# Sliding-window attention by whole chunks: both halves' scores together, all transposes together, and PSUM banks shared in turn

## The chip, the cores and the metric

The kernel runs on one core of a Trainium2 chip. Its time is the device time of one launch in microseconds (us). The engines are named as the profile names them: PE (matrix products; PEld is its weight load), DVE (vector), ACT (scalar, activation functions), POOL (a second vector engine) and SP (issues DMAs). Each engine runs its own queue in the order in which the program was laid down; engines meet through semaphores. [...]

## The reference, cut to what matters

One inference step of a one-layer hybrid encoder: retention, sliding-window attention (SWA), cross attention and a gated feed-forward block, on 1024 prompt rows and 64 sample rows, all in float32. The change lies in SWA, whose core is:

```python
SWA_HEADS = 16; SWA_KV_HEADS = 2; SWA_GROUP = 8; SWA_HD = 64; CHUNK = 64; WINDOW = 128

def swa_attend(q, k, v, bias, sinks, valid):
    s = jnp.einsum('bnqhgd,bnkhd->bnhgqk', q, k, preferred_element_type=jnp.float32) * (SWA_HD ** -0.5)
    s = s + bias.astype(jnp.float32)
    if valid is not None:
        s = jnp.where(valid, s, NEG_INF)
    sink = sinks.astype(jnp.float32)[:, :, None, None]
    m = jnp.maximum(jnp.max(s, axis=-1, keepdims=True), sink)
    e = jnp.exp(s - m)
    p = e / (jnp.sum(e, axis=-1, keepdims=True) + jnp.exp(sink - m))
    return jnp.einsum('bnhgqk,bnkhd->bnqhgd', p.astype(v.dtype), v)

a = (rms_norm(ret_o).astype(ret_g.dtype).reshape(B, S, -1) * jax.nn.silu(ret_g)) @ w_ret_out
b = swa_o.reshape(B, S, -1) @ w_swa_out
```

Each chunk of 64 queries sees 192 keys (its own chunk and the two before it; fewer at the start). There are 16 chunks of the prompt and one of the sample: 17.

## The kernel before

The SWA phase (`swa_phase`, `swa`) stands at about 808 to 990 us of the span. A chunk c is worked in two halves (`hf` 0 and 1, eight heads each). In a half, two heads of each of the two key/value groups `v` lie on 128 partitions as rows (head, query), so that a half has four units (v, i), each of 128 rows by up to 192 keys.

- `scores(c, hf)`: PE makes the scores of a half in `pss` (L972; eight rows in the trace, two banks, tag `s`, one buffer). DVE scales them by 0.125 and adds the bias (L982, or L985 for chunks 0 and 1, which have 64 and 128 keys), takes the row maxima (L987), negates and bounds them by the sinks (L988), and forms `es` (L991). ACT takes the exponentials unit by unit with their sums (L993, four times) and that of `es` (L995). DVE makes the reciprocal `den` (L996, L997), POOL multiplies the first 128 keys (L999, `t`) and the last 64 (L1004, `e`).
- `turn(c, hf)`: PE transposes the four units of `t` into `pp` (L1016, one bank, tag `pt0`) and two of `e` into another `pp` (L1027, tag `pt1`); ACT copies the first to SBUF (L1020), DVE the second (L1029). PE also transposes values (L949, copied by ACT at L951).
- `weigh(c)`, after both halves: PE multiplies with the values into `pout` (L1040, sixteen rows in the trace, two banks, tag `out`), and DVE copies the result to `osb` (L1044), which is stored.

Between these blocks PE works on `filler()`, the output projection of the retention branch: `pieces` are groups of three-pass matmuls (L156 to L158, `mm3`, `pd`), each on one of three column ranges (384, 384, 320 columns, `CH`) for one of eight weight units of `w_ret_out`. A unit's float32 weights `raw` are split by ACT (L123) and DVE (L124) into a high and a low part `wq`; the operands `ret` of a column range are split in the same way (`later_operands`, L123 and L124; `first_low`, L1113 to L1125, for the first range). A finished piece is multiplied by its gate on DVE (L1201) and stored.

`fill()` yields how many pieces come at each place: none after the scores of half 0 of chunk 0, six after half 1, then 38 spread over the 34 half steps, then eight. `in_order` ties each block to PE's last matmul, so that the program lays down, for half step i: weigh (if a chunk has ended), scores two halves ahead, turn, filler. Within such constraints a scheduler places every instruction on its engine, also those of the other engines. `step` counts the pieces of the projection; the load of weight unit 2 is issued after `first`, DVE's product of step 2.

Of the kernel before, what the change touches and what calls it, by code (L numbers as in the profile page):

```python
# [19 lines left out]
P = 128  # L20
# [89 lines left out]
class Kernel:  # L110
# [438 lines left out]
    def bias_table(self):  # L549
# [9 lines left out]
        nc.vector.tensor_copy(rb, pb[:16, :256].unsqueeze(1).broadcast_to([16, 2, 256]))  # L559
# [367 lines left out]
    def swa(self, ctx, fill):  # L927
        nc, tc, io = self.nc, self.tc, self.io
        if True:
# [26 lines left out]
            halves = [(c, hf) for c in range(17) for hf in range(2)]  # L956
# [7 lines left out]
            def scores(c, hf):  # L964
                ks, j0, nk = keys(c)
                if hf == 0 and c % 4 == 0 and 0 < c < 13:
                    self.load_queries(qTs, c + 4)
                qT = qTs[c // 4 % 2]
                pss = pw.tile([P, 2, 512], F32, tag="s", name="pss")
# [10 lines left out]
                if nk == NKEY:  # L980
                    fl = lambda x: x.rearrange("p v i n -> p v (i n)")
                    nc.vector.scalar_tensor_tensor(fl(t), pss[:, :, :2 * NKEY], 0.125, fl(bs[:, :, hf]), ALU.mult, ALU.add)  # L982
                else:
                    for v in range(2):
                        nc.vector.scalar_tensor_tensor(t[:, v, :, :nk], ps[:, v, :, :nk], 0.125, bs[:, v, hf, :, j0:],  # L985
                                                       ALU.mult, ALU.add)
                nc.vector.tensor_reduce(nm, t[:, :, :, :nk], AX.X, ALU.max)  # L987
                nc.vector.scalar_tensor_tensor(nm, nm, -1.0, quad(self.minus), ALU.mult, ALU.min)  # L988
# [3 lines left out]
                for v, i in units:  # L992
                    nc.scalar.activation(t[:, v, i, :nk], t[:, v, i, :nk], AF.Exp, bias=nm[:, v, i:i + 1],  # L993
# [14 lines left out]
            def turn(c, hf):  # L1008
                ks, j0, nk = keys(c)
                if hf == 0:  # L1010
                    live[c] = [values(ks + k0) for k0 in ((0, 64, P) if nk == NKEY else (0,))]
                (t, e), vt = live.pop((c, hf)), live[c]
                n = min(P, nk)
                pp = pw.tile([P, 512], F32, tag="pt0", name="pp")
                for j, (v, i) in enumerate(units):
                    self.last_mm = nc.tensor.transpose(pp[:n, j * P:(j + 1) * P], t[:, v, i, :n], self.ident).ins  # L1016
                if hf == 0:
                    live[c, "T"] = [self.pw2.tile([P, 2, 512], F32, tag="pT0", name="pT"), self.pw2.tile([P, 512], F32, tag="pT1", name="pT")]
                pT = live[c, "T"][0][:n]
                nc.scalar.copy(pT[:, :, hf * 256:(hf + 1) * 256], pp[:n, :].rearrange("p (v i) -> p v i", v=2))  # L1020
                cs = [slice(h * 256, (h + 1) * 256) for h in range(2)]
                parts = [[(h, v, vt[0][:n], pT[:, v, cs[h]]) for h in range(2) for v in range(2)]]
                if nk == NKEY:
                    pp = pw.tile([P, 512], F32, tag="pt1", name="pp")
                    for i in range(2):
                        x = e[:, i].rearrange("p r k -> p (r k)")
                        self.last_mm = nc.tensor.transpose(pp[:, i * P:(i + 1) * P], x, self.ident).ins  # L1027
                    pT = live[c, "T"][1]
                    nc.vector.tensor_copy(pT[:, hf * 256:(hf + 1) * 256], pp[:, :256])  # L1029
# [809 lines left out]
```

## Time and profile before

| what | value |
| --- | --- |
| median of three runs | 2186.65 us (2181.92 to 2186.86) |
| the profiled execution | 2187.39 us |
| its span | 2185.2 us, mean granted clock of PE 0.995 |
| PE busy | 2144.0 us, 98% of the span |
| DVE, ACT, POOL busy | 1566.2, 876.4, 651.6 us |
| SWA phase, 806 to 990 us | 184.00 us, PE busy in 176.75 of them |

A row of the timeline reads: start in us, duration, engine, line and operation, output and inputs with their shape, how many instructions, and in brackets the idle time before it with what ended it. A row of the groups reads: line, engine, operation, shapes and count, then busy time in us and the mean ns of one, then idle time before them with its releasers. The table of stretches has, for each stretch, its length and the busy time of each engine, then the granted clock of PE (PEclk, 1.00 is full), the share of the DMA engines and GB/s.

### The profile page before, as it was taken

How to read it: one execution, taken by the hardware profiler on the slowest of the kernel's cores; microseconds unless marked ns; L12 is line 12 of the kernel's file. 1: busy time of each engine (PE TensorE's matmuls, PEld its weight loads, DVE VectorE, ACT ScalarE, POOL GpSimd, SP SyncE). 2: the span in 40 equal slices, each digit the busy share in tenths (PEclk: the TensorE clock that was granted, in tenths of full speed). 3: DMA queues.
4: the chain of work that ended last, by engine and by line, in shares of the span. 5: the costliest groups of instructions: out<-in, count | busy, mean ns of one | idle time of the engine just before them, and what ended most of it. 6: DMA issues, size and time to landing. Idle time of an engine off the chain costs nothing.

```text
span 2185.2 us, 41707 instructions
## 1 busy us (share of the span) xinstructions
PE 2144.0 (98%) x16389; PEld 2088.9 (96%) x16389; DVE 1566.2 (72%) x2658; ACT 876.4 (40%) x1898; POOL 651.6 (30%) x498
## 2 busy tenths in 40 slices
PE   8999999999999998999999999999999999999997
PEld 8999999999999997889999999999999999999997
DVE  8996968776677658775455555768777776787588
ACT  7343424344344455653233333333322322344243
POOL 1222333332344213340000000014565555514531
PEclk9999999999999999999999999999999999999998
DMA  6434354445244567326443111422333323294333
GB/s 207 157 128 122 109 148 128 133 121 153 103 160 159 171 206 233 124 80 219 121 154 119 43 49 59 146 87 91 122 126 113 104 99 117 93 331 135 127 110 116
DMA packets 181444, 290.83 MB, mean 133 GB/s; under 512 B 40290, under 2 KB 109314, under 8 KB 181250
## 3 DMA queue, kind: packets, MB, share of 16 engines
q1 hardware_dynamic: 176130, 278.18, 39.7%
q10 hardware_dynamic: 4608, 8.36, 1.0%
q8 instruction: 129, 2.11, 0.4%
q0 software_dynamic: 512, 1.64, 0.2%
q14 instruction: 65, 0.53, 0.1%
HBM read 196.95 MB, written 91.16 MB: 132 GB/s over the span
## 4 chain that ended last, share of the span: by engine, by line
PE 78%; DVE 11%; DMA 5%; issue 2%; ACT 2%; POOL 1%; SPq 0%; POOLq 0%; DVEq 0%; ACTq 0%
PE pq L215 16%; PE pq L212 15%; PE pq L213 15%; PE pd L156 7%; PE pd L158 7%; PE pd L157 7%; DVE wq L124 2%; PE pout L1040 1%; PE pss L972 1%; DMA hl<-d_op 1%; DVE u L259 1%; PE pp L1016 1%; DVE T L124 1%; DVE B L124 1%; DMA raw<-w_k 1%
## 5 line engine op out<-in xcount | busy, mean ns | idle before, releaser
L124 DVE TENSOR_TENSOR wq<-raw,wq 128x512 fp32r<-128x512 f32 (+1 forms) x499 | 443.2, 891 | 145.0 <-ACT wq L123 142.9
L123 ACT CAST wq<-raw 128x512 fp32r<-128x512 f32 (+1 forms) x499 | 302.9, 614 | 588.2 <-PE pq L215 210.4
L212 PE MATMUL pq<-T,wq 128*128 128x272 f32 x1832 | 492.1, 288 | 4.9 <-ACT wq L123 3.2
L213 PE MATMUL pq<-T,wq 128*128 128x272 f32 x1832 | 492.9, 289 | 0.0
L213 PE MATMUL pq<-B,wq 128*128 128x272 f32 x1592 | 427.3, 288 | 3.1 <-DVE B L124 2.9
L212 PE MATMUL pq<-B,wq 128*128 128x272 f32 x1592 | 425.9, 288 | 0.7 <-DVE tok L725 0.4
L190 POOL TENSOR_TENSOR raw<-raw 128x512 f32<-128x512 f32 (+1 forms) x59 | 86.5, 1467 | 1030.5 <-DVE rs_r L301 481.0
L215 PE MATMUL pq<-T,wq 128*128 128x272 f32 x1832 | 382.7, 289 | 1.5 <-DVE wq L124 1.5
L212 PEld LDWEIGHTS pq<-T,wq 128*128 128x128 f32 x1832 | 345.0, 188 | 6.8 <-ACT wq L123 3.3
L213 PEld LDWEIGHTS pq<-T,wq 128*128 128x128 f32 x1832 | 344.6, 188 | 1.2 <-issue 1.1
L215 PE MATMUL pq<-B,wq 128*128 128x272 f32 x1592 | 331.5, 289 | 0.0
L213 PEld LDWEIGHTS pq<-B,wq 128*128 128x128 f32 x1592 | 298.8, 188 | 4.5 <-DVE B L124 4.4
L212 PEld LDWEIGHTS pq<-B,wq 128*128 128x128 f32 x1592 | 298.8, 188 | 1.7 <-issue 0.9
L215 PEld LDWEIGHTS pq<-T,wq 128*128 128x128 f32 x1832 | 290.0, 190 | 2.7 <-DVE wq L124 1.8
L215 PEld LDWEIGHTS pq<-B,wq 128*128 128x128 f32 x1592 | 251.5, 189 | 0.5 <-issue 0.4
L259 DVE TENSOR_TENSOR u<-pq,u 128x544 f32<-128x544 f32 x177 | 127.2, 719 | 92.6 <-PE pq L215 92.5
L193 POOL TENSOR_TENSOR raw<-raw 128x512 f32<-128x512 f32 (+1 forms) x59 | 80.8, 1370 | 93.4 <-DVE wq L124 83.5
L598 DVE TENSOR_TENSOR stage<-pq,u 128x544 f32<-128x544 f32 x112 | 80.3, 717 | 36.7 <-PE pq L215 33.9
L191 POOL TENSOR_TENSOR raw<-raw 128x512 f32<-128x512 f32 (+1 forms) x59 | 89.1, 1510 | 3.6
L196 POOL TENSOR_TENSOR raw<-raw 128x512 f32<-128x512 f32 (+1 forms) x59 | 86.0, 1457 | 4.4
L1488 POOL TENSOR_TENSOR stage<-stage,rstd_f 128x544 f32<-128x544 f32 x40 | 63.9, 1608 | 39.1 <-ACT stage L1487 39.1
L156 PE MATMUL pd<-xc,wq 128*128 128x256 f32 (+1 forms) x256 | 74.5, 291 | 0.0
(385 smaller groups left out, 4555.5 us busy)
## 6 DMA issues: line engine op xcount, KB each, us to landing
hl<-d_op SPq DMA_DIRECT2D x85, 272.0 KB, 5.0
d_qkv<-stage SPq DMA_DIRECT2D x44, 272.0 KB, 2.4
d_op<-stage SPq DMA_DIRECT2D x44, 272.0 KB, 2.1
d_op<-ht SPq DMA_DIRECT2D x44, 272.0 KB, 3.1
raw<-w_gate SPq DMA_DIRECT2D x22, 512.0 KB, 3.5
raw<-w_up SPq DMA_DIRECT2D x22, 512.0 KB, 3.5
raw<-w_down SPq DMA_DIRECT2D x16, 512.0 KB, 5.3
d_gate<-stage ACTq DMA_DIRECT2D x28, 272.0 KB, 3.2
```

The costliest lines, as they stand in the source:

```text
L123: self.last_cast = self.nc.scalar.copy(hi, src).ins
L124: return self.nc.vector.tensor_tensor(out=lo, in0=src, in1=hi.bitcast(F32), op=ALU.subtract).ins
L156: mm(ps, wh, xh, start=start, stop=False)
L157: mm(ps, wh, xl, start=False, stop=False)
L158: self.last_mm = mm(ps, wl, xh, start=False, stop=stop).ins
L190: tt(out=a11, in0=a11, in1=a21, op=sub)
L191: tt(out=a21, in0=a21, in1=a22, op=add)
L196: tt(out=a12, in0=a12, in1=a11, op=sub)
L212: mm(ps[:, c, :HC], w[:, 0, ks], x[:, 0, cs], start=start, stop=False)
L213: mm(ps[:, c, :HC], w[:, 0, ks], x[:, 1, cs], start=False, stop=False)
L215: self.last_mm = mm(ps[:, c, :HC], w[:, 1, ks], x[:, 0, c * HC:(c + 1) * HC], start=False, stop=stop).ins
L259: add = lambda out, a, b: nc.vector.tensor_tensor(out=out, in0=a, in1=b, op=ALU.add)
```

## The change

- The scores of both halves of a chunk are issued together, the chunk's transposes together, and the weighing stands ahead of the next scores. For chunk c the program lays down: weigh(c-1), scores(c+1), filler, turn(c), filler.
- Tag `s` has two buffers of two banks each. Scores of a half take one; all eight transposes of `t` of a chunk take the next, as one tile `pp` of two banks. The four transposes of `e` go into the upper half of the `out` tile, whose lower half later takes the weighing; one DVE copy per chunk (`rest`, L1024) takes them out in place of two. Tags `pt0` and `pt1` are gone; the phase uses as many banks as before.
- The first softmax step is one DVE operation per unit, `tensor_tensor_reduce` (L984): sum of scores and bias, times -0.125, with the running minimum kept; it is followed by a readout of one element per partition. It takes the place of L982/L985, L987 and L988. The bias table is stored times 8, and the exponential takes scale -1.
- The load of weight unit 2 is issued after the marks (`ready` and the exponential of `es`) that are the latest at step 6, in place of DVE's product of step 2.

Lines move: L972 becomes L974, L993 L990, L1016 stays, L1020 becomes L1017, L1027 L1020, L1029 L1024, L1040 L1032, L1044 L1036, L1201 L1195.

```diff
-        nc.vector.tensor_copy(rb, pb[:16, :256].unsqueeze(1).broadcast_to([16, 2, 256]))
+        nc.vector.tensor_scalar(rb, pb[:16, :256].unsqueeze(1).broadcast_to([16, 2, 256]), 8.0, None, ALU.mult)
...
-                yield []
                 yield [pieces] * 6
...
-            def scores(c, hf):
+            def scores(c):
+                if c % 4 == 0 and 0 < c < 13:
+                    self.load_queries(qTs, c + 4)
+                for hf in range(2):
+                    half_scores(c, hf)
...
-                pss = pw.tile([P, 2, 512], F32, tag="s", name="pss")
+                pss = pw.tile([P, 2, 512], F32, tag="s", bufs=2, name="pss")
...
-                if nk == NKEY:
-                    fl = lambda x: x.rearrange("p v i n -> p v (i n)")
-                    nc.vector.scalar_tensor_tensor(fl(t), pss[:, :, :2 * NKEY], 0.125, fl(bs[:, :, hf]), ALU.mult, ALU.add)
-                else:
-                    for v in range(2):
-                        nc.vector.scalar_tensor_tensor(t[:, v, :, :nk], ps[:, v, :, :nk], 0.125, bs[:, v, hf, :, j0:],
-                                                       ALU.mult, ALU.add)
-                nc.vector.tensor_reduce(nm, t[:, :, :, :nk], AX.X, ALU.max)
-                nc.vector.scalar_tensor_tensor(nm, nm, -1.0, quad(self.minus), ALU.mult, ALU.min)
+                for v, i in units:
+                    u = quad(self.minus)[:, v, i:i + 1]
+                    nc.vector.tensor_tensor_reduce(t[:, v, i, :nk], ps[:, v, i, :nk], bs[:, v, hf, i, j0:], -0.125, u,
+                                                   ALU.add, ALU.min, nm[:, v, i:i + 1])
...
-                    nc.scalar.activation(t[:, v, i, :nk], t[:, v, i, :nk], AF.Exp, bias=nm[:, v, i:i + 1],
+                    nc.scalar.activation(t[:, v, i, :nk], t[:, v, i, :nk], AF.Exp, bias=nm[:, v, i:i + 1], scale=-1.0,
...
-            def turn(c, hf):
+            def turn(c):
...
-                pp = pw.tile([P, 512], F32, tag="pt0", name="pp")
-                for j, (v, i) in enumerate(units):
-                    self.last_mm = nc.tensor.transpose(pp[:n, j * P:(j + 1) * P], t[:, v, i, :n], self.ident).ins
...
+                pp = pw.tile([P, 2, 512], F32, tag="s", bufs=2, name="pp")
+                po = pw.tile([P, 2, 512], F32, tag="out", name="pout")
+                first = self.pw2.tile([P, 2, 512], F32, tag="pT0", name="pT")[:n]
...
+                for hf in range(2):
+                    t, e = live.pop((c, hf))
+                    for j, (v, i) in enumerate(units):
+                        self.last_mm = nc.tensor.transpose(pp[:n, hf, j * P:(j + 1) * P], t[:, v, i, :n], self.ident).ins
+                    nc.scalar.copy(first[:, :, cs[hf]], pp[:n, hf, :].rearrange("p (v i) -> p v i", v=2))
+                    for i in range(2 if nk == NKEY else 0):
+                        x = e[:, i].rearrange("p r k -> p (r k)")
+                        self.last_mm = nc.tensor.transpose(po[:, hf, (2 + i) * P:(3 + i) * P], x, self.ident).ins
...
+                    nc.vector.tensor_copy(rest.rearrange("p (h i) -> p h i", h=2), po[:, :, 256:])
...
-            for i in range(-2, n):
-                if i > 0:
-                    self.in_order(lambda: weigh(*halves[i - 1]))
-                if i + 2 < n:
-                    self.in_order(lambda: scores(*halves[i + 2]))
-                if i >= 0:
-                    self.in_order(lambda: turn(*halves[i]))
...
+            self.in_order(lambda: scores(0))
...
+            filled()
+            for c in range(17):
+                if c:
+                    self.in_order(lambda: weigh(c - 1))
+                if c < 16:
+                    self.in_order(lambda: scores(c + 1))
+                filled()
+                self.in_order(lambda: turn(c))
+                filled()
...
-                        with tc.issue_after(first):
+                        with tc.issue_after(first[0]), tc.issue_after(first[1]):
...
-                if step == 2:
-                    first = ins
+                if step == 6:
+                    first = self.marks[-1]
```

PE, chunk 0's second half of transposes (`t_9799` before, `t_9796` now), in the kernel before; a row is line, operation, output and inputs with the numbers of their buffers, shape, and in brackets the engines or DMA queues whose semaphores it waits for:

```order
L156 MATMUL pd_9956<-ret3_9728,wq_9888 128x384
L157 MATMUL pd_9956<-ret3_9728,wq_9888 128x384
L158 MATMUL pd_9956<-ret3_9728,wq_9888 128x384
L972 MATMUL pss_9981<-swin0_9711,swin1_9712 128x128 [waits DVE_49,PE_49]
L972 MATMUL pss_9981<-swin0_9711,swin1_9712 128x128 x3
L1016 MATMUL pp_10003<-ident_63,t_9799 64x128 [waits Activation_49,Pool_49]
L1016 MATMUL pp_10003<-ident_63,t_9799 64x128 x3
```

and in the kernel as changed:

```order
L158 MATMUL pd_9967<-ret3_9728,wq_9888 128x384
L948 MATMUL pd_9992<-ident_63,swin5_9716 128x128 [waits DMAHW2_49,DVE_49]
L1016 MATMUL pp_9995<-ident_63,t_9774 64x128 [waits DVE_49,Pool_49]
L1016 MATMUL pp_9995<-ident_63,t_9774 64x128 x3
L1016 MATMUL pp_9995<-ident_63,t_9796 64x128 [waits Activation_49,Pool_49]
L1016 MATMUL pp_9995<-ident_63,t_9796 64x128 x3
L156 MATMUL pd_9967<-ret4_9729,wq_9891 128x384
```

Both groups of transposes now write one tile `pp_9995`, and the second, which waits for ACT's copy of the first, stands directly behind it.

ACT, around the copy of chunk 0's first transposes (`pT_9952` before, `pT_9997` now), in the kernel before:

```order
L123 COPY wq_9888<-raw_9886 128x512 [waits Activation_49]
L123 COPY wq_9891<-raw_9886 128x512 [waits Activation_49]
L123 COPY wq_10499<-raw_10497 128x512 [waits DMAHW1_49,Activation_49]
L123 COPY wq_10502<-raw_10497 128x512 [waits Activation_49]
L951 COPY swin4_9715<-pd_9944 128x128 [waits PE_49]
L1020 COPY pT_9952<-pp_9947 64x2x256 [waits PE_49]
L993 ACTIVATE t_9927,den_9933<-t_9927,nm_9928 128x128 [waits DVE_49]
L993 ACTIVATE t_9927,den_9933<-t_9927,nm_9928 128x128 x3
```

and in the kernel as changed, where row one and two are chunk 1's exponentials:

```order
L990 ACTIVATE t_9927,den_9933<-t_9927,nm_9928 128x128 [waits DVE_49] x4
L990 ACTIVATE t_9949,den_9955<-t_9949,nm_9950 128x128 [waits DVE_49] x4
L992 ACTIVATE es_9934<-es_9934 128x4 [waits DVE_49]
L992 ACTIVATE es_9956<-es_9956 128x4 [waits DVE_49]
L123 COPY ret0_9725<-swin3_9714 128x384 [waits DMAHW7_49]
L123 COPY ret1_9726<-swin3_9714 128x384 [waits DMAHW0_49]
L123 COPY ret2_9727<-swin3_9714 128x384 [waits DMAHW2_49]
L123 COPY ret3_9728<-swin6_9717 128x384 [waits DMAHW3_49]
L123 COPY ret4_9729<-swin6_9717 128x384 [waits DMAHW4_49]
L123 COPY ret5_9730<-swin6_9717 128x384 [waits DMAHW5_49]
L123 COPY ret6_9731<-swin6_9717 128x384 [waits DMAHW7_49,Activation_49]
L950 COPY swin4_9715<-pd_9992 128x128 [waits PE_49]
```

The next row is L1017's copy of the first group. The conversions of unit 2 (`wq_10499`, `wq_10502`) have left this place; they stand behind chunk 2's exponentials and four conversions of `ret`. The copy, which had stood ahead of chunk 1's exponentials, stands behind all eight of them and seven conversions.

PE, a later chunk, where the weighing begins, in the kernel before:

```order
L156 MATMUL pd_10320<-ret7_9732,wq_9752 128x320
L157 MATMUL pd_10320<-ret7_9732,wq_9752 128x320
L158 MATMUL pd_10320<-ret7_9732,wq_9752 128x320
L1040 MATMUL pout_10381<-pT_10312,swin4_9715 64x256 x2
L1040 MATMUL pout_10381<-pT_10312,swin4_9715 64x256 [waits Activation_49]
L1040 MATMUL pout_10381<-pT_10312,swin4_9715 64x256
```

and in the kernel as changed:

```order
L157 MATMUL pd_10327<-ret7_9732,wq_9752 128x320
L158 MATMUL pd_10327<-ret7_9732,wq_9752 128x320
L1016 MATMUL pp_10343<-ident_63,t_10180 128x128 [waits Activation_49]
L1016 MATMUL pp_10343<-ident_63,t_10180 128x128 x3
L1032 MATMUL pout_10344<-pT_10345,swin4_9715 64x256 [waits DVE_49]
L1032 MATMUL pout_10344<-pT_10345,swin4_9715 64x256
L1032 MATMUL pout_10344<-pT_10345,swin4_9715 64x256 [waits Activation_49]
L1032 MATMUL pout_10344<-pT_10345,swin4_9715 64x256
```

Before, filler stood between the last transposes and the weighing; now the second group of transposes stands directly ahead of it, and the weighing's third row waits for ACT's copy of that group.

More of the change, by code (lines that the diff above doesn't have):

```diff
@@ L955, in swa @@
             units = [(v, i) for v in range(2) for i in range(2)]
-            halves = [(c, hf) for c in range(17) for hf in range(2)]
             live, outs = {}, {}
@@ L1006, in scores @@
                 live[c, hf] = t, e
-            def turn(c, hf):
+            def turn(c):
                 ks, j0, nk = keys(c)
-                if hf == 0:
-                    live[c] = [values(ks + k0) for k0 in ((0, 64, P) if nk == NKEY else (0,))]
-                (t, e), vt = live.pop((c, hf)), live[c]
+                vt = [values(ks + k0) for k0 in ((0, 64, P) if nk == NKEY else (0,))]
                 n = min(P, nk)
-                pp = pw.tile([P, 512], F32, tag="pt0", name="pp")
-                for j, (v, i) in enumerate(units):
[L1016 to L1020, printed above, removed]
-                cs = [slice(h * 256, (h + 1) * 256) for h in range(2)]
-                parts = [[(h, v, vt[0][:n], pT[:, v, cs[h]]) for h in range(2) for v in range(2)]]
-                if nk == NKEY:
[L1024 to L1029, printed above, removed]
-                    parts.append([(h, r ^ h, vt[2 - r][rows[r]], pT[rows[r], cs[h]]) for h in range(2) for r in (h, 1 - h)])
-                live[c, "parts"] = parts
@@ new lines, in turn, with weigh @@
+                parts = [[(h, v, vt[0][:n], first[:, v, cs[h]]) for h in range(2) for v in range(2)]]
+                if nk == NKEY:
+                    rest = self.pw2.tile([P, 512], F32, tag="pT1", name="pT")
+                    nc.vector.tensor_copy(rest.rearrange("p (h i) -> p h i", h=2), po[:, :, 256:])
+                    parts.append([(h, r ^ h, vt[2 - r][rows[r]], rest[rows[r], cs[h]]) for h in range(2) for r in (h, 1 - h)])
+                live[c] = parts, po
+            def weigh(c):
+                parts, po = live.pop(c)
```

24 lines of the change are left out of this document (8 added, 16 removed).

## The prediction, made before the changed kernel was run

> **What bounds the kernel now.** I read the busy time of each engine over the whole span first, then the same in stretches of the one phase that the change touches, then PE's list of instructions there, and last ACT's and DVE's where PE stood still.
>
> ```profile
> PE 2144.0 (98%) x16389; PEld 2088.9 (96%) x16389; DVE 1566.2 (72%) x2658; ACT 876.4 (40%) x1898; POOL 651.6 (30%) x498
> core 0: us, PE busy (x) PEld busy (x) DVE busy (x) ACT busy (x) POOL busy (x), PEclk, DMA share, GB/s
> 806.00:820.00 14.00, 12.47 (x90) 11.84 (x88) 7.83 (x22) 12.59 (x36) 4.11 (x8) 0.88 0.56 189
> 820.00:840.00 20.00, 16.10 (x102) 13.61 (x100) 15.06 (x37) 9.42 (x32) 3.73 (x4) 0.91 0.86 281
> 880.00:900.00 20.00, 20.00 (x155) 16.37 (x154) 16.72 (x37) 13.16 (x52) 7.58 (x12) 1.00 0.44 136
> 806.00:990.00 184.00, 176.75 (x1298) 144.64 (x1297) 134.20 (x320) 111.00 (x408) 64.33 (x101) 0.98 0.46 145
> ```
>
> PE bounds it: 98% of the span, and 176.75 of the 184 us of this phase. So the change can win at most 184 - 176.75 = 7.25 us of idle time, the clock lost around it, and the small gaps between blocks. DVE leaves 184 - 134.2 = 49.8 us free, ACT 73. In the later stretch PE never stops. The idle time sits at the start:
>
> ```profile
> 809.67 0.66 PE L972 MATMUL pss<-swin,swin 64*128 64x64 f32 x8 [0.68 <-DVE t L985]
> 822.42 0.71 PE L972 MATMUL pss<-swin,swin 64*128 64x128 f32 x8
> 823.24 0.60 PE L1016 MATMUL pp<-ident,t 128*64 128x128 f32 x4
> 823.59 0.42 PE L156 MATMUL pd<-ret,wq 128*128 128x384 f32 x1
> 825.62 0.34 PE L158 MATMUL pd<-ret,wq 128*128 128x384 f32 x1
> 829.85 0.72 PE L972 MATMUL pss<-swin,swin 64*128 64x128 f32 x8 [3.90 <-DVE t L985]
> 831.46 0.52 PE L157 MATMUL pd<-ret,wq 128*128 128x384 f32 x1
> 834.02 0.41 PE L156 MATMUL pd<-ret,wq 128*128 128x384 f32 x1
> 827.10 1.14 ACT L123 CAST wq<-raw 128x512 fp32r<-128x512 f32 x2 [7.82 <-DMA raw<-w_ret_out]
> 828.96 0.75 DVE L985 SCALAR_TENSOR_TENSOR t<-pss,swin 128x256 f32<-128x256 f32 x2
> ```
>
> The 3.90 us wait is a chain: weight unit 2 came late from memory (ACT waited 7.82 us), DVE's half of that conversion stands in its queue ahead of chunk 1's first softmax step (828.96), and PE needs that step to free its only scores bank. After it eight matmuls took 834.02 - 831.46 = 2.56 us, 0.32 each; the twelve from 823.59 to 825.62 took 2.03/11 = 0.185 each. So about 1.4 us more went to a lower clock (0.91 granted in that stretch).
>
> **What the change removes.** Unit 2's conversions now stand behind chunk 2 in both queues, so 3.90 goes. The second scores bank removes 0.68. The 0.61 below (PE waiting for an ACT copy behind four exponentials) and the POOL waits of 0.84 and 0.31 go too, since chunk c is turned 1.5 chunks after its scores instead of one. Together 3.90 + 1.40 + 0.68 + 0.61 + 1.15 = 7.7 us.
>
> ```profile
> 845.93 0.66 PE L1016 MATMUL pp<-ident,t 128*128 128x128 f32 x4 [0.84 <-POOL t L999]
> 846.89 0.44 PE L1027 MATMUL pp<-ident,e 128*128 128x128 f32 x2 [0.31 <-POOL e L1004]
> 861.84 0.65 PE L1040 MATMUL pout<-pT,swin 128*64 128x256 f32 x4
> 863.11 1.25 PE L1040 MATMUL pout<-pT,swin 128*64 128x256 f32 x12 [0.61 <-ACT pT L1020]
> 862.49 0.56 ACT L1020 COPY pT<-pp 128x512 f32<-128x512 f32 x1
> ```
>
> **What it adds on DVE.** Per half chunk, three operations become four units of a new 192-element operation, each with a one-element readout.
>
> ```profile
> L993 ACT ACTIVATE t<-t,nm 128x192 f32<-128x192 f32 x120 | 53.1, 443 | 25.6 <-DVE nm L988 23.9 <-DVE es L991 1.0 <-DVE den L997 0.7
> L982 DVE SCALAR_TENSOR_TENSOR t<-pss,swin 128x768 f32<-128x768 f32 x30 | 28.6, 952 | 5.1 <-PE pss L972 4.9
> L987 DVE TENSOR_REDUCE nm<-t 128x4 f32<-128x768 f32 x30 | 28.3, 943 | 0.0
> L988 DVE SCALAR_TENSOR_TENSOR nm<-nm,minus 128x4 f32<-128x4 f32 x34 | 5.7, 168 | 0.6
> L985 DVE SCALAR_TENSOR_TENSOR t<-pss,swin 128x256 f32<-128x256 f32 x4 | 1.5, 416 | 0.0
> L985 DVE SCALAR_TENSOR_TENSOR t<-pss,swin 128x128 f32<-128x128 f32 x4 | 1.0, 286 | 0.0
> L987 DVE TENSOR_REDUCE nm<-t 128x4 f32<-128x512 f32 x2 | 1.4, 685 | 0.1
> L987 DVE TENSOR_REDUCE nm<-t 128x4 f32<-128x256 f32 x2 | 0.8, 420 | 0.1
> ```
>
> No row shows the operation. From L985, 128 more elements cost 416 - 286 = 130 ns, so 156 ns are fixed and 192 elements are 351 ns; the readout is at most like L988's 168. At 519 ns a unit, 136 units are 70.6 us, against 28.6 + 28.3 + 5.7 + 1.5 + 1.0 + 1.4 + 0.8 = 67.3 now. Bounds: at 952/4 + 0 a unit it saves 35 us of DVE, and up to 49.8 us more is covered by DVE's free time. I take nothing on PE's path. Merging the `rest` copies saves DVE a little, likewise covered.
>
> [...]
>
> **What it adds on PE, chunk 0.** Both halves' transposes now write one tile, back to back, and the second four wait until ACT has copied the first four. In between nothing hides that copy, and in ACT's queue it stands behind all eight exponentials of chunk 1 and seven conversions of `ret`.
>
> ```profile
> 822.90 0.54 DVE L1201 TENSOR_TENSOR swin<-pd,swin 128x384 f32<-128x384 f32 x1
> 830.66 0.40 ACT L993 ACTIVATE t<-t,nm 128x128 f32<-128x128 f32 x1 [1.78 <-DVE nm L988]
> 832.21 0.19 ACT L995 ACTIVATE es<-es 128x4 f32<-128x4 f32 x1
> 832.31 1.74 ACT L123 CAST ret<-swin 128x384 fp32r<-128x384 f32 x4
> L951 ACT COPY swin<-pd 128x128 f32<-128x128 f32 x18 | 4.7, 264 | 10.8 <-PE pd L949 10.8
> ```
>
> PE: chunk 1's scores begin at 822.42 - 0.68 = 821.7, take 2 x 0.65, twelve matmuls 2.2, transposes 0.5; the second four are due near 825.7. DVE is busy until 822.90 + 0.54 = 823.4, so the first unit is done near 823.8. DVE makes units at most every 0.45 us and ACT takes them every (832.21 - 830.66)/4 = 0.39, so the eighth exponential ends near 827.3. Then es twice 0.2, seven conversions at 1.74/4 = 0.43, 3.0, a values copy of 0.2 (at most 0.26) and the copy of 0.56 (row 862.49): 831.2. PE waits about 5.5 us (5.0 where DVE's units come quicker than ACT takes them). The lower clock after it, 1.4, I keep as in the kernel before.
>
> **Chunk 1.** The same order returns. From 831.2: transposes 0.45, twelve slower matmuls 3.4, the weighing and both scores halves 1.0 + 1.7, twelve matmuls 2.1, transposes 0.45, so the second four are due at 840.3. The first half's scores are done at 836.8; eight exponentials at 0.443 make 3.5, then the queue holds 0.2, four conversions of 320 columns and unit 2's pair, then the copy:
>
> ```profile
> 845.48 1.52 ACT L123 CAST ret<-swin 128x320 fp32r<-128x320 f32 x4
> 891.80 1.68 PE L1040 MATMUL pout<-pT,swin 128*64 128x256 f32 x16
> 893.40 0.92 PE L972 MATMUL pss<-swin,swin 64*128 64x192 f32 x8
> 894.42 0.60 PE L1016 MATMUL pp<-ident,t 128*128 128x128 f32 x4
> 894.86 0.38 PE L1027 MATMUL pp<-ident,e 128*128 128x128 f32 x2
> 895.11 0.59 ACT L1020 COPY pT<-pp 128x512 f32<-128x512 f32 x1 [0.23 <-PE pp L1016]
> ```
>
> 836.8 + 0.5 + 3.5 + 0.2 + 1.52 + 1.14 + 0.6 = 844.3, a wait of 4.0 us; 2 if the conversions can run early, 5 if their loads land late. The clock after it: 0 to 1.4, I take 1.2.
>
> [...]
>
> **Chunks 2 to 16.** The wait is hidden by matmuls that now stand between the two groups of transposes; but the second group stands straight ahead of the weighing, whose third row reads its copy. From the first of four transposes (894.42) the copy starts after 0.69 (895.11) and takes 0.59, and PE goes on 0.06 after a copy's end (862.49 + 0.56, 863.11): 1.34. PE's next block starts after 0.44 (894.86), and four passes lie before the waiting row at 1.60/16 = 0.10 each (891.80 to 893.40): 0.84. I take the difference, 0.5 us a chunk; bounds 0 (the scheduler's matmuls reach PE earlier) and 0.9 (a conversion of 0.43 queued ahead of the copy). Fifteen chunks: 7.5 us. Against it, one scores block and one transposes block per chunk instead of two each saves a few gaps, 0.1 to 0.2: 17 x 0.13 = 2.2 us.
>
> **The sum.** -7.7 + 5.5 + 1.4 (chunk 0) + 4.0 + 1.2 (chunk 1) + 7.5 - 2.2 = +9.7 us. The profiled execution took 2187.39 us (span 2185.2), 0.74 above the median of the runs, 2186.65. 2187.4 + 9.7 = 2197.1; on the median's footing 2196.4, which I forecast.
>
> **Rivals.**
> 1. Only the early waits come; the copies of later chunks are hidden. Then 9.7 - 7.5 = +2.2: 2188.9. For it: ACT has 73 us free and the copy itself is short. Against: 0.61 us was lost at 863.11 in that place when the copy was late.
> 2. Faster: the two early waits are together under 2.5 us, because ACT starts its conversions before the exponentials are ready or DVE's units are short, and the clock holds; with no waits in later chunks, -7.7 + 2.5 - 2.2 = -7.4: 2179.3. It decides from early waits below 2.5 us. Against it: an engine's queue runs in order, and twelve or more operations stand ahead.
> 3. DVE becomes the bound: a unit with readout at 1.1 us makes 136 x 1.1 = 150 us, 82 more than now against 49.8 free: +32 and some 5 us of the early waits, near 2224. It decides from (67.3 + 49.8)/136 = 0.86 us. Against it: every DVE row here fits 156 ns and 1 ns an element.
> 4. The waits are longer: each ACT copy stands behind one more conversion (0.43 to 0.57) in most of the later chunks, 15 x 0.5 = 7.5: 2204. For it: two conversions of weights come in many chunks, and ACT runs in order. Against: those copies have matmuls of about 4 us ahead of them.
>
> **How the numbers follow.** The likeliest course 0.55 (its own range 2190 to 2203); rival 1 0.14, rival 2 0.13, rival 3 0.06, rival 4 0.12. About 0.3%, 6.6 us, is what a measurement of this kernel tells from no change: faster is below 2180.1, slower above 2193.2. Faster: rival 2, 0.13. Same: rival 1 and a fifth of the likeliest, 0.25. Slower: the rest, 0.62. The range 2181 to 2207 leaves out rival 3, most of rival 2 and a little of rival 4.
>
> **What would show it.** Right: in the changed kernel's PE list a wait of 4 us or more ahead of the second group of L1016 in chunks 0 and 1, released by ACT's L1017, and about 0.5 us ahead of L1032 in most later chunks, with no wait on DVE's scores step near 826. The DVE units at L984 should read about 350 ns. Wrong: units over 0.8 us with PE waiting on DVE at L974; PE's busy time unbroken from 840 on; or the first waits under 2 us, which would make the forecast's sign wrong.

## The result, and the profile after

The changed kernel took 2194.26 us, the median of six runs (2189.27 to 2195.73), against 2185.47 us (2181.92 to 2186.86) for the kernel before in six runs beside them: a ratio of 1.0037, 95% interval 1.0025 to 1.0049. It is slower by 8.8 us, of which the interval allows 5.5 to 10.7. The forecast was 2196.4.

The stretches of the phase after (columns as in the prediction):

```profile
820.00:840.00 20.00, 15.73 (x98) 13.39 (x96) 13.29 (x51) 10.84 (x42) 3.31 (x4) 0.83 0.45 146
840.00:860.00 20.00, 15.77 (x104) 12.46 (x106) 15.40 (x41) 11.06 (x40) 8.95 (x12) 0.91 0.84 267
880.00:900.00 20.00, 19.73 (x152) 16.02 (x149) 12.78 (x60) 11.77 (x48) 7.38 (x12) 1.00 0.38 118
```

In the stretch of 840 to 860 us PE had been busy for 18.85 of the 20 us; now it is for 15.77, and its clock is 0.91. PE's timeline names the waits:

```profile
816.98 0.45 PE L156 MATMUL pd<-ret,wq 128*128 128x384 f32 x1 [1.47 <-ACT swin L1166]
824.74 0.60 PE L1016 MATMUL pp<-ident,t 128*64 128x128 f32 x4
829.54 1.03 PE L1016 MATMUL pp<-ident,t 128*64 128x128 f32 x4 [4.21 <-ACT pT L1017]
843.94 0.63 PE L1016 MATMUL pp<-ident,t 128*128 128x128 f32 x4 [4.00 <-ACT pT L1017]
```

The 3.90 us wait on DVE is gone; in its place PE waits 4.21 and 4.00 us for ACT's copy between the two groups of transposes of chunks 0 and 1. The wait of 1.47 us ahead of them is for L1166, where ACT scales a result of the values projection (816.47, `swin<-pd,mtok`) and so frees its bank of PSUM, which PE writes and ACT reads (the same line is L1172 in the order before). ACT's timeline around chunk 0's copy shows what it stood behind: the last of chunk 1's exponentials, the two of `es`, seven conversions, then the copy.

```profile
825.22 0.39 ACT L990 ACTIVATE t<-t,nm 128x128 f32<-128x128 f32 x1
825.60 0.28 ACT L992 ACTIVATE es<-es 128x4 f32<-128x4 f32 x2
825.79 2.97 ACT L123 CAST ret<-swin 128x384 fp32r<-128x384 f32 x7
828.67 0.25 ACT L950 COPY swin<-pd 128x128 f32<-128x128 f32 x1
828.83 0.58 ACT L1017 COPY pT<-pp 64x512 f32<-64x512 f32 x1
```

PE had reached the second group at about 825.3; without the seven conversions, by an estimate from these rows (825.79 + 829.41 - 828.67), the copy would have been done near 826.5.

In a later chunk (PE's timeline, and ACT's row between):

```profile
876.39 0.60 PE L1016 MATMUL pp<-ident,t 128*128 128x128 f32 x4
876.92 1.99 PE L1032 MATMUL pout<-pT,swin 128*64 128x256 f32 x16
878.84 1.41 PE L974 MATMUL pss<-swin,swin 64*128 64x192 f32 x14
877.03 0.58 ACT L1017 COPY pT<-pp 128x512 f32<-128x512 f32 x1 [1.82 <-PE pp L1016]
```

The weighing takes 878.84 - 876.92 = 1.92 us to the next block, where it took 1.60 before: 0.32 us of waiting. The idle column shows none of it here and at most 0.17 in other chunks; the rest lies within the merged row, which is 1.99 us long where the row of before (891.80) is 1.68. The copy runs from 877.03 to 877.61, within the weighing.

DVE's new operation and its readout, as groups:

```profile
L984 DVE CUSTOM_DVE_ANT_0 t<-pss,swin,minus 128x192 f32<-128x192 f32 x120 | 42.9, 414 | 3.7 <-PE pss L974 3.7
L984 DVE DVE_READ_ACCUMULATOR2_ANT nm<- 128x1 f32 x136 | 11.3, 83 | 0.0
```

Busy time of a row overlaps that of its neighbours: in the timeline the units start 0.34 us apart, readout included (898.34, 898.68, 899.02 in one half).

Below, the phase is measured from the start of the first scores to the start of the last weighing, and cut where the weighing of chunk 2 starts. All numbers are differences of start times in the profiled executions.

| kernel | first scores to chunk 2 | chunk 2 to chunk 16 | sum | median of all runs | ratio to before, 95% |
| --- | --- | --- | --- | --- | --- |
| before | 44.94 | 133.05 | 177.99 | 2185.47 | |
| before, second profile | 43.36 | 133.10 | 176.46 | | |
| changed | 48.69 | 135.05 | 183.74 | 2194.26 | 1.0037 (1.0025 to 1.0049) |
| changed, second profile | 52.24 | 135.14 | 187.38 | | |
| two tiles | 41.69 | 130.97 | 172.66 | 2181.75 | 0.9983 (0.9974 to 0.9992) |
| unit 2 alone | 45.03 | 133.83 | 178.86 | 2184.51 | 1.0004 (0.9993 to 1.0016) |
| old softmax in the new order | 50.40 | 156.69 | 207.09 | 2212.51 | 1.0125 (1.0111 to 1.0138) |
| copies first | 42.40 | 136.71 | 179.11 | 2189.14 | 1.0020 (1.0009 to 1.0032) |
| two tiles and copies first | 38.33 | 133.65 | 171.98 | 2180.57 | 0.9986 (0.9975 to 0.9996) |
| new softmax in the old order | 42.77 | 132.02 | 174.79 | 2183.60 | 0.9997 (0.9988 to 1.0006) |
| old place of unit 2 | 49.38 | 135.00 | 184.38 | 2190.95 | 1.0031 (1.0019 to 1.0042) |
| two tiles, old softmax | 45.90 | 148.40 | 194.30 | 2204.37 | 1.0098 (1.0083 to 1.0114) |
| values' scaling first | 37.13 | 133.76 | 170.89 | 2182.15 | 0.9991 (0.9982 to 0.9999) |

The ratios go by the kernel before, run beside each kernel on the same chip, whose median was 2184.56 beside the first four experiments, 2183.67 beside the next four and 2183.80 beside the last.

### The profile page after: what moved, and what is told of

Same layout as the page of the kernel before. It is cut to its first block, busy times and chain, and to the rows that moved or that the text cites. A ratio compares the mean times of both kernels' runs of the same rounds, so it can differ in the third digit from the quotient of the medians.

```text
span 2193.5 us, 41793 instructions
## 1 busy us (share of the span) xinstructions
PE 2145.9 (98%) x16389; PEld 2092.0 (95%) x16389; DVE 1553.9 (71%) x2809; ACT 873.4 (40%) x1898; POOL 649.8 (30%) x498
## 5 line engine op out<-in xcount | busy, mean ns | idle before, releaser
L124 DVE TENSOR_TENSOR wq<-raw,wq 128x512 fp32r<-128x512 f32 (+1 forms) x499 | 448.7, 903 | 158.2 <-ACT wq L123 156.6
L190 POOL TENSOR_TENSOR raw<-raw 128x512 f32<-128x512 f32 (+1 forms) x59 | 85.2, 1445 | 1040.8 <-DVE rs_r L301 485.1
L193 POOL TENSOR_TENSOR raw<-raw 128x512 f32<-128x512 f32 (+1 forms) x59 | 80.7, 1368 | 93.3 <-DVE wq L124 83.4
L191 POOL TENSOR_TENSOR raw<-raw 128x512 f32<-128x512 f32 (+1 forms) x59 | 87.5, 1484 | 3.6
L196 POOL TENSOR_TENSOR raw<-raw 128x512 f32<-128x512 f32 (+1 forms) x59 | 83.9, 1423 | 4.4
L990 ACT ACTIVATE t<-t,nm 128x192 f32<-128x192 f32 (+2 forms) x136 | 58.8, 434 | 51.6 <-DVE nm L984 51.6
```

Of the source, the lines that this page charges most:

```text
L124: return self.nc.vector.tensor_tensor(out=lo, in0=src, in1=hi.bitcast(F32), op=ALU.subtract).ins
L190: tt(out=a11, in0=a11, in1=a21, op=sub)
L191: tt(out=a21, in0=a21, in1=a22, op=add)
L193: tt(out=a11, in0=a22, in1=a11, op=sub)
L196: tt(out=a12, in0=a12, in1=a11, op=sub)
```

## The experiments

### Two tiles in place of one

```diff
-                pss = pw.tile([P, 2, 512], F32, tag="s", bufs=2, name="pss")
+                pss = [pw.tile([P, 512], F32, tag="s%d" % v, bufs=2, name="pss") for v in range(2)]
...
-                pp = pw.tile([P, 2, 512], F32, tag="s", bufs=2, name="pp")
+                pps = [pw.tile([P, 512], F32, tag="s%d" % hf, bufs=2, name="pp") for hf in range(2)]
```

The same four banks, but each is a tile of its own, so that the second transposes no longer wait for the copy of the first. The scores of a half now lie in two tiles as well.

> The changed kernel with each pair of banks of tag s held as two tiles of one bank, so that the two halves' transposes go to two tiles; all else as changed. Theory (the second transposes wait for ACT's copy of the first because they write one tile): the waits of 4.21 and 4.00 us ahead of L1016 are gone; what remains of them moves to the weighing of chunks 0 and 1 (about 2.9 and 1.8 us, since ACT's copies still stand behind eight exponentials and the conversions); the weighing of later chunks takes 1.60 again in place of 1.92. About 2182 us, 12 less than the changed kernel, some 3 less than the kernel before. Rival (the wait belongs to ACT's queue, not to the shared tile): the same 4 us appear ahead of the weighing and the time stays within 3 us of 2194. Rival (DVE's new operation sets the time): no change.

Measured: 2181.75 us, faster than both kernels, as the theory said. PE's timeline at the weighing of chunk 0, and one later chunk:

```profile
830.04 0.65 PE L1032 MATMUL pout<-pT,swin 64*64 64x256 f32 x4 [1.52 <-ACT pT L1017]
830.93 1.12 PE L1032 MATMUL pout<-pT,swin 64*64 64x256 f32 x4 [0.24 <-ACT pT L1017]
888.05 1.68 PE L1032 MATMUL pout<-pT,swin 128*64 128x256 f32 x16
889.66 1.57 PE L974 MATMUL pss<-swin,swin 64*128 64x192 f32 x16
```

Both 4 us waits are gone, 1.76 us of the first shows up at the weighing (2.9 was expected), none of the second (1.8 was expected), and a later weighing takes 889.66 - 888.05 = 1.61 again. The scheduler also moved the second transposes back ahead of the filler, which now hides the copy. So both the early and the later loss come from the second group's dependence on the first group's copy. Splitting the tile of the scores is not what helped: from chunk 4 to 15 they take 1.50 us a chunk with either.

### Copies ahead of the conversions

```diff
-        with self.tc.issue_after(a), self.tc.issue_after(b):
+        with self.tc.issue_after(a), self.tc.issue_after(b), self.tc.issue_after(self.copied):
...
-            extra = {2: (1, 0), 3: (1, 1), 5: (2, 0), 7: (2, 1)}
+            extra = {3: [(1, 0), (1, 1)], 5: [(2, 0)], 7: [(2, 1)]}
```

`copied` is the last L1017 of a chunk, and the first four conversions are asked for one step later; the shared tile stays.

> The changed kernel with ACT's conversions of ret issued behind the chunk's copies (L1017) in place of ahead of them, the one shared tile kept. Theory (the early waits are the copy's place in ACT's queue): the 4.21 us falls to about 1.1 and the 4.00 to about 1.2, and the lower clock behind each goes, 2184 to 2188 us; the weighing of later chunks still takes 1.92. Rival (the conversions are needed at once by PE, so the wait moves to L156): waits of 2 to 4 us ahead of L156 at chunks 1 and 2 and 2191 us or more.

Measured: 2189.14 us, a little more than expected. Of the changed kernel's loss 3.7 us are back by the ratios (1.0020 beside 1.0037), 5.1 by the medians. The profiled run, 2194.52 us, was the slowest of its twelve. PE's timeline:

```profile
829.85 0.60 PE L1016 MATMUL pp<-ident,t 128*64 128x128 f32 x4 [1.28 <-ACT pT L1017]
839.69 0.63 PE L1016 MATMUL pp<-ident,t 128*128 128x128 f32 x4 [1.16 <-ACT pT L1017]
862.85 0.66 PE L1016 MATMUL pp<-ident,t 128*128 128x128 f32 x4 [1.88 <-ACT pT L1017]
```

The two waits fell to 1.28 and 1.16 as forecast. A new one of 1.88 at chunk 3 and two of 0.78 near 851 us give part of it back. The one long wait ahead of L156, 2.81 us at 820.17, is for L1166 and lies ahead of the conversions that were moved, so that rival falls. The weighing of later chunks still takes 1.93 us. The place in ACT's queue sets how long the early waits are; the shared tile makes them waits at all.

### Both together

> Both experiments before together: two tiles of one bank for the transposes, and ACT's conversions of ret behind the chunk's copies. Theory (the two causes add up to all of the early waits): the waits of 1.52 and 0.24 us at the weighing of chunk 0 that two tiles left go too, later chunks as with two tiles: 2179 us, 2 to 3 less than two tiles alone. Rival (with two tiles the copies are no longer late, and the conversions behind them only make PE's L156 wait): 2182 us or more.

Measured: 2180.57 us, the lowest median of the study, but not to be told from two tiles alone by these intervals. ACT's timeline at chunk 0, then PE's largest wait:

```profile
823.76 1.06 ACT L1017 COPY pT<-pp 64x512 f32<-64x512 f32 x2
824.71 3.41 ACT L123 CAST ret<-swin 128x384 fp32r<-128x384 f32 x8
856.18 1.68 PE L1032 MATMUL pout<-pT,swin 128*64 128x256 f32 x16 [1.67 <-DVE pT L1024]
```

The waits of 1.52 and 0.24 us at chunk 0's weighing are gone, as the theory said. Up to chunk 2 the profile is 3.4 us shorter than that of two tiles, but not by these waits alone: the wait for L1166 is 0.9 us shorter, a stretch of lower clock in the other profile (matmuls 0.32 us apart from 835.33 to 837.57, and 0.175 from 837.78 on) is missing here, and three new waits of 0.78, 0.52 and 0.67 us for DVE's softmax stand ahead of L1016. Up to chunk 16 2.7 us come back, 1.67 of them on DVE's copy of the `e` transposes. The time shows no gain, so the theory's 2 to 3 us did not come.

### Unit 2's load moved, in the order before

```diff
-                        with tc.issue_after(first):
+                        with tc.issue_after(first[0]), tc.issue_after(first[1]):
...
-                if step == 2:
-                    first = ins
+                if step == 6:
+                    first = self.marks[-1]
```

> The kernel before with one part of the change alone: the load of weight unit 2 is issued after the marks of step 6. Theory: the wait of 3.90 us on DVE at chunk 1 and about 1.4 us of lower clock after it go, nothing else moves: 2180 us, 5 less than before. Rival (the wait only moves to the next place that needs DVE or ACT, or to unit 2's first use): within 2 us of 2185.5.

Measured: 2184.51 us against 2184.56: no gain clear of noise (the interval goes from 1.5 us less to 3.5 more). PE's timeline holds what came in place of the 3.90, and ACT's what the longest of the later ones stood behind:

```profile
821.03 0.69 PE L156 MATMUL pd<-ret,wq 128*128 128x384 f32 x1 [2.79 <-ACT swin L1172]
841.62 0.66 PE L1016 MATMUL pp<-ident,t 128*128 128x128 f32 x4 [1.20 <-POOL t L999]
849.38 0.44 PE L156 MATMUL pd<-ret,wq 128*128 128x384 f32 x1 [2.13 <-ACT swin L951]
861.28 0.92 PE L972 MATMUL pss<-swin,swin 64*128 64x192 f32 x8 [0.67 <-DVE t L982]
848.03 1.13 ACT L123 CAST wq<-raw 128x512 fp32r<-128x512 f32 x2
```

The rival holds by the time: the wait goes, and others come. The 2.13 us one ends with L951, which stands right behind unit 2's two conversions in their new place. The 2.79 us one lies ahead of everything that the edit moves; it differs from run to run (nothing and 0.75 us in the two profiles of the kernel before). With it came 2.6 us of lower clock (matmuls 0.32 us apart from 821.52 to 826.96, and 0.175 behind them), and the profiled run, 2189.86 us, is among the slowest of its twelve. The three later waits, less the 0.84 and 0.31 us of POOL waits that they replace, make 2.9 of the 5.1 us that went (3.90 and 1.2 of clock); one profile does not settle the rest.

### Unit 2's old place, in the new order

The same edit undone in the changed kernel.

> The changed kernel with the load of weight unit 2 issued after DVE's product of step 2, as before. Theory (unit 2's late conversion then holds DVE ahead of chunk 1's softmax, so that the exponentials and the copies behind them come later by 5 us): the wait at L1016 of chunk 0 grows from 4.2 to about 8 us, the one of chunk 1 shrinks by about 1.1, time 2197 to 2199 us. Rival (as in the old order, moving unit 2 is worth nothing): 2193 to 2195 us.

Measured: 2190.95 us, a ratio of 1.0031 beside 1.0037 for the changed kernel: again no difference clear of noise, and the theory falls. DVE's and PE's timelines:

```profile
824.05 1.28 DVE L124 TENSOR_TENSOR wq<-raw,wq 128x512 fp32r<-128x512 f32 x2
831.44 0.60 PE L1016 MATMUL pp<-ident,t 128*64 128x128 f32 x4 [3.95 <-ACT pT L1017]
843.87 0.63 PE L1016 MATMUL pp<-ident,t 128*128 128x128 f32 x4 [3.00 <-POOL e L1001]
```

Unit 2's weights were there in time (824.05, where the kernel before had them converted at 827.75), so DVE did not wait for them, and the wait at L1016 stayed at 4 us. On ACT they were converted from 818.38, against 827.10 in the kernel before; why they came so much earlier is not shown, and the late arrival on which the theory rests was thus not tried in the new order. The second wait fell by 1.00, as expected of two conversions fewer ahead of the copy; POOL's `e` now ends it.

### The old softmax in the new order

> The changed kernel with the three old softmax operations in place of the new one per unit. Theory (DVE's number of operations costs nothing; the new form helps, as ACT can begin its exponentials after the first unit, 0.35 us, and not after the whole half, 1.6 to 2.1 us): the waits ahead of L1016 grow by 1 to 1.6 us each in chunks 0 and 1, time 2196 to 2198 us. Rival (the new operations cost time on DVE that PE waits for): 2190 us or less. Rival (hidden both ways): within 1 us of 2194.

Measured: 2212.51 us, 18 to 19 more than the changed kernel, and far outside what any side expected. One chunk, with DVE's, ACT's and PE's rows:

```profile
899.07 0.96 DVE L984 SCALAR_TENSOR_TENSOR t<-pss,swin 128x768 f32<-128x768 f32 x1 [0.21 <-PE pss L974]
900.06 0.95 DVE L989 TENSOR_REDUCE nm<-t 128x4 f32<-128x768 f32 x1
900.93 0.95 DVE L984 SCALAR_TENSOR_TENSOR t<-pss,swin 128x768 f32<-128x768 f32 x1
901.79 0.15 DVE L990 SCALAR_TENSOR_TENSOR nm<-nm,minus 128x4 f32<-128x4 f32 x1
901.91 0.95 DVE L989 TENSOR_REDUCE nm<-t 128x4 f32<-128x768 f32 x1
902.85 0.55 DVE L1200 TENSOR_TENSOR swin<-pd,swin 128x384 f32<-128x384 f32 x1
902.04 0.46 ACT L995 ACTIVATE t<-t,nm 128x192 f32<-128x192 f32 x1 [5.24 <-DVE nm L990]
903.46 0.41 PE L156 MATMUL pd<-ret,wq 128*128 128x320 f32 x1 [0.59 <-DVE swin L1200]
907.53 0.65 PE L1037 MATMUL pout<-pT,swin 128*64 128x256 f32 x4 [1.03 <-ACT pT L1022]
```

Four long operations of a chunk now stand in one line on DVE. The first exponential starts at 902.04, three us after the first of them (899.07); the small operation that it needs (901.79) stands in DVE's queue behind the second half's first long one. With the new form ACT begins 0.46 us after the first unit (898.34 to 898.80 in the changed kernel). Behind the long operations stand the gate product that frees PE's bank (0.59 us) and, on ACT, the copies behind the eight late exponentials (1.03 us). From chunk 2 on PE waits 7.9 us in all for such copies ahead of the weighing, 2.3 ahead of the transposes, and 5.9 for the gate product; its clock from 860 to 980 us is 0.95, where the changed kernel has 1.00. DVE is not full: 77.15 of these 120 us are busy, against 79.65 in the changed kernel. So it is the length of the chain and the order in the queue, not the load; which of the two weighs more is not shown.

### The old softmax with two tiles

The first operation is done once per group `v`, 128x384 twice.

> Two tiles of one bank, with the old softmax operations (the first of them once per group v, 128x384 twice in place of 128x768). Theory (with both halves' scores together, DVE's two long operations per half hold back the exponentials, ACT's copies and the gate product that frees PE's bank, whatever the tiles are): 8 to 16 us more than two tiles with the new softmax, 2190 to 2198 us, with waits on DVE's gate product ahead of L156 of about 0.6 us in most chunks. Rival (the old softmax was dear only through the shared tile): within 3 us of 2182.

Measured: 2204.37 us, 23 to 25 more than two tiles with the new softmax. The loss is thus not one of the shared tile; it came out larger than the 8 to 16 expected. Waits on DVE's gate product ahead of L156 are there, of 0.27 to 0.66 us, in some chunks and not in most. The larger ones come ahead of the weighing: 3.25 us once on DVE's copy of the `e` transposes, and ACT's copies again, up to 1.77 us in the later chunks and 4.03 in chunk 1.

### The new softmax in the old order

> The kernel before with the new softmax operation alone, in the old order. Theory (DVE is not on the path in the old order, where each half has its own place and the exponentials have a chunk's time): 2182 to 2185 us, the 3.90 us wait within 0.7 of what it was, since unit 2 still stands ahead. Rival (the new operation is worth the 18 us that its removal cost in the new order): 2170 us or less.

Measured: 2183.60 us against 2183.67, no difference, as the theory said. But the wait at chunk 1 was shorter than it allowed, in PE's timeline:

```profile
827.90 0.87 PE L972 MATMUL pss<-swin,swin 64*128 64x128 f32 x8 [2.29 <-DVE nm L982]
```

Up to the last weighing the profile is 3.2 us shorter than the one of before, or 1.7 than its second one; the medians show none of it.

### The scaling of the values projection first

```diff
-            self.in_order(lambda: scores(0))
+            self.in_order(lambda: half_scores(0, 0))
...
+            for pieces in start[:2]:
+                self.in_order(lambda: next(pieces, None))
+            with tc.issue_after(self.values_out):
+                self.in_order(lambda: half_scores(0, 1))
```

Added to two tiles and copies first.

> Two tiles and copies first, and in chunk 0 the second half's scores and softmax laid down behind the first piece of the values projection, so that ACT's two scalings of that projection (L1166 of the changed kernel) stand ahead of the second half's exponentials. Theory (PE waits for the first of these scalings, as it frees a bank, and ACT does all eight exponentials of chunk 0 first): the wait ahead of L156 near 816 us, 1.24 us with two tiles and copies first and 1.47 in the changed kernel, goes: 2179 us, about 1 us less. Rival (the second half's softmax, now behind DVE's conversions, makes chunk 0's transposes late): a new wait of 1 to 3 us ahead of L1016 near 825 us, 2181 us or more.

Measured: 2182.15 us, not faster than without it. The wait near 816 is gone and no new one came at 825; the phase is 1.1 us shorter in the profile. The time does not follow: behind the last weighing this profile has 1202.7 us, the other 1199.5. Why it is not faster stays open.

### Both kernels again

> The changed kernel itself, profiled a second time. The question is the part of the profiled difference that lies outside the phase: 183.74 - 177.99 = 5.75 us of the 8.3 us lie between the first scores and the last weighing, and 2.3 behind it. Theory (what lies behind is scatter of the same instructions): the phase repeats to 0.5 us, 183.2 to 184.3, and the stretch behind the last weighing, 1201.2 us in the first profile and 1198.9 before, comes out elsewhere between 1198 and 1203. Rival (the change costs 2.3 us behind the phase): 1201 to 1201.5 again.

> The kernel before, profiled a second time, for the same question. Theory (scatter): the phase repeats, 177.5 to 178.5 us, and the stretch behind the last weighing differs from 1198.9 by 1 us or more. Rival: both repeat to 0.3 us.

Neither phase repeats as closely as expected. From chunk 2 on both do, to 0.1 us; the start does not: the changed kernel took 3.6 us longer up to chunk 2, the kernel before 1.6 less. PE's timeline of the changed kernel's second profile:

```profile
817.20 0.69 PE L156 MATMUL pd<-ret,wq 128*128 128x384 f32 x1 [2.86 <-ACT swin L1166]
832.46 0.60 PE L1016 MATMUL pp<-ident,t 128*64 128x128 f32 x4 [4.18 <-ACT pT L1017]
846.31 0.63 PE L1016 MATMUL pp<-ident,t 128*128 128x128 f32 x4 [4.38 <-ACT pT L1017]
```

The two waits for the copies repeat; what varies is how late ACT's scaling L1166 comes and the clock after it. In the kernel before it is a stretch of lower clock near 811 us, worth 1.3 us, that only the first profile has (its rows are in the last section). Behind the last weighing the four profiles left 1198.9 and 1198.0 us (before), 1201.3 and 1199.1 (changed), so the 2.3 us by which the first pair differed there did not repeat. The mean of the two pairs, 185.56 - 177.23 = 8.3 us, lies in the phase and agrees with the 8.8 of the medians.

## Why the prediction was right

**What it rested on** held. The waits were where the text put them, with the releaser that it named: 4.21 and 4.18 us at chunk 0 where it had 5.5, 4.00 and 4.38 at chunk 1 where it had 4.0. Two tiles took both away, and moving the copies in ACT's queue cut them to 1.28 and 1.16. At chunk 0 the forecast was long because it let DVE be busy until 823.4 and the units follow at 0.45 us; the first unit started at 822.11 and they follow at 0.27. (Its terms there, 827.3 + 0.4 + 3.0 + 0.2 + 0.56, make 831.5 and not the 831.2 written, so the wait should have read 5.8.) The lower clock behind each wait came too: 1.45 and 1.06 us in the first profile, 1.24 and 1.47 in the second, where 1.4 and 1.2 were forecast. The 1.4 was read behind the 3.90 us wait of the kernel before; the 1.2 was the author's estimate, and no row of that kernel shows it.

**The later chunks**: 0.5 us a chunk was forecast for the copy, 0.32 was measured (1.92 against 1.60). The saving of 0.13 was met as a sum, not in its parts. From chunk 4 to 15, with the same filler matmuls in both, a chunk went from 9.36 to 9.55 us on the mean, so 0.32 - 0.19 = 0.13 was saved: two scores blocks of 0.85 became one of 1.50, which with the filler and the values' transposes saves 0.32, while the transposes of `t` and `e` take 1.40 in place of 1.22. From chunk 2 to 16 the forecast's terms make 14 x 0.37 - 0.61 = +4.6; measured were +2.0 in both pairs. This term was mis-sized.

**Moving unit 2** was priced at 3.90 + 1.40 us of gain. That step does not hold as a price: alone the move gave nothing clear of noise (1.0004, interval 0.9993 to 1.0016), and undone in the changed kernel it cost nothing. In the order before, other waits on ACT, POOL and DVE came up when the 3.90 us were taken away; in the new order the weights came in time from the old place too, so it is not shown that the move is what took the wait away there.

**The second scores bank** did remove its 0.68, but ACT's scaling L1166 then set the time. From the first scores PE reached the filler behind that scaling after 6.98 us in both profiles of the changed kernel, 9.41 and 7.87 before, and went on after 8.45 and 9.84, against 9.44 and 8.62 before. So the waits of 1.47 and 2.86 us, which the sum did not have, took up what was won, and in the second profile 2.5 us of lower clock followed. To chunk 2 the forecast's terms make some +5; measured were +3.8 and +8.9.

That the sum came so near, +9.7 against a measured +8.8, is therefore partly luck: the later chunks were 2.6 us too dear in it, the start 1.3 us too cheap on the mean of the two pairs, and the pairs themselves lie 5 us apart. The sign is not luck, since two tiles alone remove the whole loss.

**DVE's new operation** was forecast to cost PE nothing, and it shows no cost (the third rival falls: where 351 ns and at most 168 were estimated, 414 and 83 were measured, 0.34 us apart, well under the 0.86 from which it would have decided). The reason given, 49.8 us of free time on DVE, was the wrong measure: with the old operations DVE had as much to spare and the time was 18 us worse. In the old order either form does as well. The prediction had no term for how much the new order needs the short first unit; a count of free time cannot show that.

Of the other rivals, the first (later copies hidden) and the second (early waits under 2.5 us) fall by the traces; of the fourth (an additional conversion ahead of each later copy) no wait is seen. A DVE unit does have a part that does not grow with its length: 345 ns for 128 elements and 414 for 192 leave, by an estimate from these two, some 207 ns, more than the 156 that the forecast took from L985. Still, four short operations beat two long ones in the new order, by 18 to 19 us: ACT began 0.46 us after the first unit started, and with the long ones 3 us after the first of them.

## What to carry to other kernels

Two groups of writes to one tile made the second wait for the reader of the first here, by 4.21 and 4.00 us, though they lie in different banks; give each group its own tile, or put enough work between them. When blocks are moved together, look at the queue of the engine that reads their result: here the whole next block (eight exponentials), and what the scheduler found ready (seven conversions, 2.97 us), stood ahead of the one operation that was waited for. Removing the largest wait of the start-up stretch, 3.90 us, alone left the time where it was (2184.51 against 2184.56), as others came up, so price such a wait by an experiment and not by its length; and judge an engine off the path by the time to its first result, not by its free time (DVE was busy for 77.15 of 120 us with the old softmax, 79.65 with the new, and the old was 18 us slower).

## What the runs showed of the hardware

PE's lower clock did not follow the length of a wait. A wait of 2.86 us in the changed kernel's second profile was followed by matmuls 0.32 us apart for some 5 us, one of 2.81 us at the same place with copies first by none:

```profile
817.68 0.52 PE L157 MATMUL pd<-ret,wq 128*128 128x384 f32 x1
818.00 0.52 PE L158 MATMUL pd<-ret,wq 128*128 128x384 f32 x1
820.17 0.45 PE L156 MATMUL pd<-ret,wq 128*128 128x384 f32 x1 [2.81 <-ACT swin L1166]
820.46 0.34 PE L157 MATMUL pd<-ret,wq 128*128 128x384 f32 x1
820.63 0.33 PE L158 MATMUL pd<-ret,wq 128*128 128x384 f32 x1
```

The first two rows are of the changed kernel's second profile, the last three of copies first. Between the two profiles of the changed kernel this is 2.5 us (seventeen matmuls at 0.32 in place of 0.175). Even short waits stood ahead of it. The kernel before waits 0.82 and 0.68 us ahead of its first two scores blocks, and the 3.5 us behind them got a clock of 0.54 in one profile and 1.00 in the other; the first row is of the first profile, the second of the second:

```profile
810.00:813.50 3.50, 3.50 (x21) 3.43 (x20) 1.40 (x6) 3.48 (x8) 1.21 (x3) 0.54 0.45 166
811.00:814.50 3.50, 3.50 (x33) 3.43 (x34) 1.67 (x7) 3.06 (x5) 1.08 (x2) 1.00 0.70 257
```

Unit 2 alone has the same two waits, 0.82 and 0.68 us, with matmuls 0.12 us apart behind them, where the first row's are 0.21 apart. So the lower clock came behind waits under 1 us in one run and not in another, and did not come behind the 2.81 us. What decides between them is not shown.
